# A hybrid decoder layer: inverse norms spread by transpositions, one partial sum of squares of x, and all steps in a new order

## The chip, the cores and the metric

The kernel runs on one core of a Trainium2 chip. The metric is the time of one execution on the device in microseconds (us). A core has a matrix engine (TensorE, in profile rows PE, with its weight loads as PEld), VectorE (DVE), ScalarE (ACT), GpSimd (POOL) and SyncE (SP), which here issues the DMA transfers. Each runs its own queue of instructions in order, and waits for the others by semaphores.

## The reference

One decoder layer over x (1 x 512 x 1024, float32): a normalised input goes through one combined projection, four heads of differential attention and eight heads of sparse attention in three branches run on it, their outputs are mixed by one projection and added to x, and a SwiGLU block with 2816 hidden columns follows.

```python
def rms_norm(x, g):
    y = xf * lax.rsqrt(jnp.mean(xf * xf, axis=-1, keepdims=True) + NORM_EPS)
    return (y * g.astype(jnp.float32)).astype(x.dtype)
...
    o_diff = diff_attention(dq, dk, dv, lam)
    o_diff = (rms_norm(o_diff, diff_subln) * (1.0 - lam_init)).reshape(B, S, DIFF_WIDTH)
...
        h = rms_norm(x, attn_pre_norm[l])
        mix = hybrid_mixer(h, ...)
        x = x + rms_norm(mix, attn_post_norm[l])
        h = rms_norm(x, ffn_pre_norm[l])
        f = (jax.nn.silu(h @ w_gate[l]) * (h @ w_up[l])) @ w_down[l]
        x = x + rms_norm(f, ffn_post_norm[l])
```

Two of these norms bear on the change: the first one, over the 1024 columns of x, and the one over the 128 columns of each differential head's output.

## The kernel before

*Number format.* Most products are float32 products made of three products of a reduced format (`fp32r`): each operand is split into a high part (ScalarE, `whi`, `xh`, `pth`) and a remainder (VectorE or GpSimd, `wlo`, `xl`, `ptl`), and high x high, high x low and low x high are summed in PSUM. A few small products are taken in float32 directly, `ssum`, `rb`, `rsb` and `ms` among them. `tr` (L867) transposes probabilities, `trc` (L1034) those of the compressed branch and `trh` (L1303) the normalised rows ahead of SwiGLU; these are `pe.transpose`.

*The stages, by the time of the profile.* Up to about 150 us: x comes in transposed (eight tiles of 128 columns by 512 tokens), is multiplied with the projection weights, and the results are rotated (rope) and written to DRAM for later. The pieces of the products of weight blocks 4 and 5 (`fm4`, `fm5`, L506) and the v products (`v`, L640) need no norm, since the norm's factor of a token is put in later: into the rope tables (`scale_rope`, L452) and into v (`dv`, L657/L660). From about 150 to 262 us the attention heads run, interleaved: D0 to D3 are differential, N0 to N7 sparse. Scores `sc` (L836 to L842), maxima `nm` (L846, DVE), exponentials `p` with their sums `l` (L850, ACT), inverses of `l` (L1007, DVE), gating of `l` and scaling of `p` (L1011, L1015, POOL), transposition, split into `pth` (L877, ACT) and `ptl` (L880, DVE), and the products with the values `avn` (L1046) or `av` (L925). Some output projections (`mixp`, L1113) are taken between, the last (`mix`, L1127) follow. From 262 to about 305 us come the norms around the residual, on VectorE above all (`pre`, L1273), while TensorE begins the SwiGLU products. From there to 622 us TensorE works through these (`yz` and `x`, L1380) and the down products (`acc`, L1454, L1602); weights stream in and are split. The last norm follows, to 635 us.

*The norm of x.* ScalarE squares x tile by tile in place (`square_x`, L392), and `add_x` (L395) sums the squares: the even tiles into the first and the odd tiles into the second, 6 additions of 128 x 512. `row_sums` (L440) lets TensorE sum each over the partitions, by products with a column of ones: for each of 4 blocks of 128 tokens two products, `ssum`. `row_norms` takes the inverse root (L294 to L303) to `rstd`, a column per token block. The factor must then stand along the rows of tiles in which tokens run along the free dimension: `row_spread` (L449) does it with 4 products of `rstd`, broadcast to 128 columns, and the identity, `rb`.

*The norm of a differential head.* Squares (`sq`), sums by `ms` (L939), `dr` (L943 on DVE, L971 on ACT, and `newton` on POOL, L947 to L950), and `spread` (L955), again 4 products with the identity, `rsb`. `ML` (L974) multiplies the output with it.

*The order.* Every step is a short function under a name, in `ops`. Three tables of such names (`PLAN`, `PLAN_NORM`, `PLAN_END`) give the order in which they are called, and that is the order of the instructions in each engine's queue:

```python
    plan = PLAN.split()
    assert sorted(plan) == sorted(ops), set(plan) ^ set(ops)
    ctx.enter_context(tc.manual_schedule())
    for tok in plan:
        ops[tok]()
```

In these names `xS3` is the square of x tile 3, `xA3` its addition, `rs` is `row_sums`, `rn` `row_norms`, `rb` `row_spread`, `F0.0` to `F0.2` the three products of weight block 0, `fh0` and `fl0` the split of its weights (L510, L515), and `D3RB` the spread of head D3. Buffers are given out from pools of fixed size (three weight tiles of each kind, for example), so the order also decides when a buffer becomes free.

Of the kernel before, what the change touches and what calls it, by code (L numbers as in the profile page):

```python
# [248 lines left out]
def hybrid_block_kernel(  # L249
# [144 lines left out]
    def add_x(k):  # L394
        dve.tensor_tensor(sqs[k % 2], sqs[k % 2], sqs[k], OP.add)  # L395
# [1526 lines left out]
```

## Time and profile before

| | us |
|---|---|
| median of 3 runs | 637.15 (636.68 to 637.2) |
| the profiled execution | 636.96 |
| its span | 635.1 |
| TensorE busy in it | 623.4 |
| VectorE busy | 549.7 |
| ScalarE busy | 373.6 |
| GpSimd busy | 97.6 |

The span is what the profiler shows of the instructions; 1.9 us of the execution lie around it. The mean granted clock of TensorE is 0.998 of full speed. In rows with "x8" that number counts records of instructions; a row's duration can overlap that of the next, since products are pipelined. The chain is followed back from the last instruction, at each step to what released it, and so its pieces add up to the span.

### The profile page before, as it was taken

How to read it: one execution, taken by the hardware profiler on the slowest of the kernel's cores; microseconds unless marked ns; L12 is line 12 of the kernel's file. 1: busy time of each engine (PE TensorE's matmuls, PEld its weight loads, DVE VectorE, ACT ScalarE, POOL GpSimd, SP SyncE). 2: the span in 40 equal slices, each digit the busy share in tenths (PEclk: the TensorE clock that was granted, in tenths of full speed). 3: DMA queues.
4: the chain of work that ended last, by engine and by line, in shares of the span. 5: the costliest groups of instructions: out<-in, count | busy, mean ns of one | idle time of the engine just before them, and what ended most of it. 6: DMA issues, size and time to landing. Idle time of an engine off the chain costs nothing.

```text
span 635.1 us, 11068 instructions
## 1 busy us (share of the span) xinstructions
PE 623.4 (98%) x4130; PEld 567.1 (89%) x4130; DVE 549.7 (87%) x965; ACT 373.6 (59%) x782; POOL 97.6 (15%) x151
## 2 busy tenths in 40 slices
PE   8999999999999999999999999999999999999995
PEld 5988888898899988888999999999999998888884
DVE  5599787989789875799999989899999999999877
ACT  6346357367788877567667555454554575566422
POOL 0200000006676868600000000000000000000000
PEclk9999999999999999999999999999999999999999
DMA  7567887453242314244133332445542554467603
GB/s 267 168 191 289 267 284 265 169 185 148 84 151 100 100 45 189 84 165 152 67 134 103 129 111 90 133 150 159 173 124 93 166 158 150 161 190 251 217 19 116
DMA packets 33045, 98.41 MB, mean 155 GB/s; under 512 B 4192, under 2 KB 5344, under 8 KB 32096
## 3 DMA queue, kind: packets, MB, share of 16 engines
q1 hardware_dynamic: 32992, 97.72, 45.9%
q8 instruction: 32, 0.52, 0.3%
q14 instruction: 21, 0.17, 0.1%
HBM read 82.10 MB, written 15.60 MB: 154 GB/s over the span
## 4 chain that ended last, share of the span: by engine, by line
PE 84%; DVE 9%; ACT 2%; issue 2%; POOL 1%; DMA 1%; SPq 0%; DVEq 0%; ACTq 0%; POOLq 0%
PE yz L1380 29%; PE acc L1454 14%; PE fm L523 12%; PE x L1380 4%; PE v L640 3%; PE acc L1602 3%; PE avn L1046 2%; PE tr L867 2%; PE g L640 2%; PE sc L836 2%; PE fm L506 2%; PE sc L837 2%; PE mixp L1113 1%; PE cmp L739 1%; DVE nm L846 1%
## 5 line engine op out<-in xcount | busy, mean ns | idle before, releaser
L850 ACT ACTIVATE p<-sc,nm 128x128 f32<-128x128 f32 (+3 forms) x96 | 50.4, 532 | 10.0 <-DVE nm L846 9.0
L846 DVE TENSOR_REDUCE nm<-sc 128x1 f32<-128x128 f32 (+3 forms) x96 | 43.8, 480 | 7.0 <-PE sc L842 5.3
L1380 PE MATMUL yz<-rope,wbh 128*128 128x256 f32 x352 | 49.0, 282 | 0.0
L1015 POOL TENSOR_TENSOR p<-p,l 128x256 f32<-128x256 f32 (+3 forms) x64 | 45.0, 726 | 0.9
L1380 PEld LDWEIGHTS yz<-rope,wbh 128*128 128x128 f32 x352 | 44.9, 189 | 0.0
L880 DVE TENSOR_TENSOR ptl<-tr,pth 128x384 fp32r<-128x384 f32 (+1 forms) x60 | 35.0, 596 | 9.4 <-ACT pth L877 9.0
L877 ACT ACTIVATE pth<-tr 128x384 fp32r<-128x384 f32 (+1 forms) x60 | 30.1, 529 | 10.1 <-PE tr L867 8.9
L836 PE MATMUL sc<-kst,qst 128*128 128x128 f32 (+3 forms) x96 | 32.6, 354 | 0.8 <-DVE ptl L880 0.4
L1357 ACT ACTIVATE weh<-e 128x1024 fp32r<-128x1024 f32 x22 | 23.3, 1058 | 15.7 <-DVE e L1339 15.2
L510 ACT ACTIVATE whi<-wraw 128x1024 fp32r<-128x1024 f32 x14 | 14.8, 1059 | 28.4 <-PE fm L523 15.7
L867 PE MATMUL tr<-ident,p 128*128 128x128 f32 x200 | 29.7, 274 | 0.8 <-POOL p L1015 0.8
L837 PE MATMUL sc<-kst,qst 128*128 128x128 f32 (+3 forms) x96 | 30.2, 322 | 0.0
L1365 DVE TENSOR_TENSOR wbl<-wraw,wbh 128x1024 fp32r<-128x1024 f32 x22 | 26.8, 1219 | 2.0 <-ACT wbh L1357 1.5
L1380 PE MATMUL yz<-rope,wbl 128*128 128x256 f32 x176 | 28.1, 282 | 0.0
L1365 DVE TENSOR_TENSOR wlo<-wraw,whi 128x1024 fp32r<-128x1024 f32 x22 | 26.7, 1219 | 1.6 <-ACT whi L1357 1.6
L523 PE MATMUL fm<-xh,whi 128*128 128x512 f32 x112 | 28.0, 393 | 0.0
L1390 ACT ACTIVATE snap<-yz 128x256 f32<-128x256 f32 x22 | 8.4, 384 | 33.0 <-PE yz L1380 32.9
L523 PE MATMUL fm<-xh,wlo 128*128 128x512 f32 x112 | 27.8, 390 | 0.0
L523 PE MATMUL fm<-xl,whi 128*128 128x512 f32 x112 | 27.8, 390 | 0.0
L1365 DVE TENSOR_TENSOR wel<-e,weh 128x1024 fp32r<-128x1024 f32 x22 | 26.8, 1217 | 0.9 <-ACT weh L1357 0.6
L1503 ACT ACTIVATE whi<-wraw 128x1024 fp32r<-128x1024 f32 x20 | 20.9, 1053 | 10.8 <-PE acc L1454 6.7
L1357 ACT ACTIVATE whi<-wraw 128x1024 fp32r<-128x1024 f32 x22 | 23.0, 1052 | 6.9 <-PE x L1380 4.8
(377 smaller groups left out, 1990.6 us busy)
## 6 DMA issues: line engine op xcount, KB each, us to landing
wraw<-in_wg SPq DMA_DIRECT2D x24, 512.0 KB, 3.4
wraw<-in_wu SPq DMA_DIRECT2D x22, 512.0 KB, 3.4
wraw<-in_wd SPq DMA_DIRECT2D x22, 512.0 KB, 3.6
wraw<-in_wf SPq DMA_DIRECT2D x14, 512.0 KB, 5.7
qk<-rope SPq DMA_DIRECT2D x7, 1024.0 KB, 5.3
kst<-qk SPq DMA_DIRECT2D x24, 256.0 KB, 4.2
wraw<-in_wo SPq DMA_DIRECT2D x8, 512.0 KB, 4.0
qst<-qk SPq DMA_DIRECT2D x16, 256.0 KB, 2.9
```

Source lines behind the costliest of these rows:

```text
L523: pe.matmul(st["fm", m], fms[m][w][:, k * P:(k + 1) * P], xx[k], start=(c == 0 and k == 0), stop=(c == 2 and k == NK - 1))
L836: pe.matmul(sv[i], lhs, kk[:, 0, :w], start=(n == 0), stop=False, skip_group_check=True)
L837: pe.matmul(sv[i], lhs, kk[:, 1, :w], start=False, stop=False, skip_group_check=True)
L846: dve.tensor_reduce(nm[i], sv[i], AX.X, OP.max, negate=True)
L850: act.activation(pp[i], sv[i], AF.Exp, bias=nm[i], accum_out=hs["l"][:, row, i:i + 1])
L867: pe.transpose(tr[:, n * P:(n + 1) * P], pp[i][:, j * P:(j + 1) * P], ident)
L880: dve.tensor_tensor(part(u, 1), tv[u], f32(part(u, 0)), OP.subtract)
L1015: pool.tensor_tensor(p, p, hs["l"][:, 1 + br, i:i + 1].to_broadcast(list(p.shape)), OP.mult)
L1357: act.activation(t[0], w[src], AF.Copy)
L1365: dve.tensor_tensor(t[1], W[f][PARTS[n][0]], f32(t[0]), OP.subtract)
L1380: pe.matmul(o, W[f][w][wi][:, k * P:(k + 1) * P], hop[h][hi][:, k * HS:(k + 1) * HS], start=(n < 3 and m == 0), stop=(m == 11), skip_group ...
L1454: pe.matmul(acc[t], a[x][:, t * P:(t + 1) * P], b[y], start=(first and n == 0), stop=(last and n == 2))
```

## The change

The two float32 products that spread a column by means of the identity become transpositions. The second partial sum of squares is added to the first on VectorE (a new step `xA1`), and `row_sums` needs one product for each token block. All three tables of the order are written anew.

```diff
     def add_x(k):
-        dve.tensor_tensor(sqs[k % 2], sqs[k % 2], sqs[k], OP.add)
+        j = k % 2 if k > 1 else 0
+        dve.tensor_tensor(sqs[j], sqs[j], sqs[k], OP.add)
...
-        if k > 1:
+        if k:
             op(f"xA{k}", add_x, k)
...
     def row_sums():
         st["ssum"] = ps("ssum")
         for i in range(NT):
-            for j in range(2):
-                pe.matmul(st["ssum"][:, i:i + 1], sqs[j][:, i * P:(i + 1) * P], ones, start=(j == 0), stop=(j == 1))
+            pe.matmul(st["ssum"][:, i:i + 1], sqs[0][:, i * P:(i + 1) * P], ones, start=True, stop=True)
...
     def row_spread():
-            pe.matmul(st["rb"][:, i * P:(i + 1) * P], rstd[:, i:i + 1].to_broadcast([P, P]), ident, start=True, stop=True)
+            pe.transpose(st["rb"][:, i * P:(i + 1) * P], rstd[:, i:i + 1].to_broadcast([P, P]), ident)
...
         def spread():
-                pe.matmul(hs["rb"][:, i * P:(i + 1) * P], hs["r"][3][:, i:i + 1].to_broadcast([P, P]), ident,
-                          start=True, stop=True)
+                pe.transpose(hs["rb"][:, i * P:(i + 1) * P], hs["r"][3][:, i:i + 1].to_broadcast([P, P]), ident)
...
 PLAN = """
-xS6 cc v0p2.1 v0p1.1 xS5 xA5 xS0 xA2 xS7 xA4 fL1 rL3 KP0 xA6 fL0 LW0 W0a xA7 rs F5.0.7 fh0 K21 F5.0.5 F4.1.5 rL2
+xA5 rL3 rL0 xA7 xA1 lL v0p3.1 v0p1.1 fh0 fl0 rs F0.0 F4.2.4
```

In the rows that follow, a name's number is that of a buffer's use, and "x4" four instructions alike; what is in a row's arrow is output and inputs.

TensorE's queue from the sums of squares to the first spread, before:

```order
L440 MATMUL ssum_413<-ones_90,xraw_160 128x1 x8
L506 MATMUL fm5_166<-xh7_312,whi_134 128x512
L506 MATMUL fm5_166<-xh5_296,whi_134 128x512
L506 MATMUL fm4_168<-xh5_296,wlo_175 128x512
L506 MATMUL fm5_166<-xl6_279,whi_134 128x512
L506 MATMUL fm5_166<-xh3_192,whi_134 128x512
L506 MATMUL fm4_168<-xh4_285,whi_158 128x512
L506 MATMUL fm4_168<-xh6_277,whi_158 128x512
L449 MATMUL rb_461<-ident_83,rstd_92 128x128 x4
L523 MATMUL fm0_466<-xh0_200,whi_423 128x512
L523 MATMUL fm0_466<-xh1_164,whi_423 128x512
```

and now (`fm0` is the first product of weight block 0, which stood behind the spread before):

```order
L440 MATMUL ssum_425<-ones_90,xraw_162 128x1 x4
L523 MATMUL fm0_430<-xh0_203,whi_421 128x512
L523 MATMUL fm0_430<-xh1_164,whi_421 128x512
L523 MATMUL fm0_430<-xh2_181,whi_421 128x512
L523 MATMUL fm0_430<-xh3_192,whi_421 128x512
L523 MATMUL fm0_430<-xh4_265,whi_421 128x512
L523 MATMUL fm0_430<-xh5_299,whi_421 128x512
L523 MATMUL fm0_430<-xh6_269,whi_421 128x512
L523 MATMUL fm0_430<-xh7_310,whi_421 128x512
L506 MATMUL fm4_172<-xl4_271,whi_160 128x512
L506 MATMUL fm4_172<-xh4_265,whi_160 128x512
L449 MATMUL rb_464<-ident_83,rstd_92 128x128 x4
```

Four products of sums instead of eight, and ten products instead of seven between these and the spread, eight of which need the high part of block 0's weights (`whi_421`); all of block 0's first product has moved ahead of the spread.

GpSimd's queue behind the last gate (`l`, L1011) of the last sparse head, up to the Newton steps of the last differential head, D3, before:

```order
L1015 TENSOR_TENSOR p_2971<-p_2971,l3_2850 128x128
L1015 TENSOR_TENSOR p_3303<-p_3303,l3_2850 128x256
L1015 TENSOR_TENSOR p_3110<-p_3110,l3_2850 128x384
L1015 TENSOR_TENSOR p_3301<-p_3301,l3_2850 128x384
L1015 TENSOR_TENSOR p_2957<-p_2957,l3_2850 128x256
L1069 TENSOR_TENSOR ol6_3277<-opair_3033,oh6_3276 128x512
L1015 TENSOR_TENSOR p_3296<-p_3296,l3_2850 128x512
L1015 TENSOR_TENSOR p_3294<-p_3294,l3_2850 128x128
L947 TENSOR_TENSOR dr_3362<-dr_3361 128x4
L948 TENSOR_TENSOR dr_3362<-dr_3362,dr_3360 128x4
L949 TENSOR_SCALAR dr_3362<-dr_3362 128x4
L950 TENSOR_TENSOR dr_3363<-dr_3361,dr_3362 128x4
```

and now (line numbers of this part are one less than before, since `spread` lost a line):

```order
L1014 TENSOR_TENSOR p_3318<-p_3318,l3_2865 128x256
L1014 TENSOR_TENSOR p_3321<-p_3321,l3_2865 128x384
L1014 TENSOR_TENSOR p_3323<-p_3323,l3_2865 128x128
L1014 TENSOR_TENSOR p_3314<-p_3314,l3_2865 128x512
L1100 TENSOR_TENSOR wl1_3423<-wraw_3134,wh1_3176 128x512
L1028 TENSOR_TENSOR pcs_3266<-pc_2952,pcs_3266 128x4x64
L947 TENSOR_TENSOR dr_3392<-dr_3391 128x4
L948 TENSOR_TENSOR dr_3392<-dr_3392,dr_3390 128x4
L949 TENSOR_SCALAR dr_3392<-dr_3392 128x4
L950 TENSOR_TENSOR dr_3393<-dr_3391,dr_3392 128x4
```

The gate is followed by four scalings instead of five and two, the remainder `wl` and the compressed branch's `pcs` (L1028, L1029 before) now stand ahead of the Newton steps, and an `ol` stands no longer there.

TensorE's queue around the spread of D3, before:

```order
L1046 MATMUL avn_3428<-pth_3395,vn0_1571 128x512
L1046 MATMUL avn_3428<-ptl_3396,vn0_1571 128x512
L955 MATMUL rsb_3437<-ident_83,dr_3363 128x128 x4
L867 MATMUL tr_3443<-ident_83,p_3303 128x128
L867 MATMUL tr_3443<-ident_83,p_3301 128x128
L867 MATMUL tr_3443<-ident_83,p_3296 128x128
L1034 MATMUL trc_3449<-ident_r_84,pcs_3338 128x128 x4
L1046 MATMUL avn_3428<-pth_3395,vn1_1613 128x384
L1046 MATMUL avn_3428<-ptl_3396,vn1_1613 128x384
L1046 MATMUL avn_3428<-pth_3395,vn2_1568 128x256
L1046 MATMUL avn_3428<-ptl_3396,vn2_1568 128x256
L1046 MATMUL avn_3428<-pth_3395,vn3_1562 128x128
```

and now:

```order
L1045 MATMUL avn_3355<-ptl_3343,vn2_1548 128x256
L1045 MATMUL avn_3355<-pth_3342,vn3_1523 128x128
L1045 MATMUL avn_3355<-ptl_3343,vn3_1523 128x128
L867 MATMUL tr_3425<-ident_83,p_3323 128x128
L867 MATMUL tr_3425<-ident_83,p_3318 128x128
L867 MATMUL tr_3425<-ident_83,p_3321 128x128
L867 MATMUL tr_3425<-ident_83,p_3314 128x128
L1033 MATMUL trc_3433<-ident_r_84,pcs_3266 128x128 x4
L955 MATMUL rsb_3442<-ident_83,dr_3393 128x128 x4
L1045 MATMUL avn_3447<-pth_3403,vn0_1464 128x512
L1045 MATMUL avn_3447<-ptl_3404,vn0_1464 128x512
```

The spread stood ahead of the last three transpositions and those of `pcs` (`trc`), behind the first two products of the last `avn`; now it stands behind all transpositions and ahead of all products of the last `avn`.

More of the change, by code (lines that the diff above doesn't have):

```diff
@@ new lines @@
+sum_ff.6.2 sum_ff.6.4 sums.3 high_ff.5.e low_ff.1.d block.1.4 high_ff.5.d high_ff.6.e low_ff.6.e low_ff.5.e
+high_ff.7.a block.5.6 high_ff.4.d gate_c.1 mult.1 snap_1.6 sum_x.6 sum_ff.6.3 low_ff.7.a high_ff.6.b block.5.5
+block.7.1 snap_1.7 sums.2 block.6.5 low_ff.5.d block.7.2 block.6.6 load_ff.7.u sum_ff.7.1 sum_ff.7.3 low_ff.6.b
+load_ff.8.g high_ff.7.b low_ff.7.b block.3.4 snap_2.5 block.5.3 sum_ff.7.2 low_ff.2.d sum_ff.7.4 snap_2.6
+high_ff.7.e block.6.3 high_ff.7.d sums.4 high_ff.6.d block.2.4 low_ff.7.e block.7.6 high_ff.8.a load_ff.8.u
@@ new lines @@
+low_ff.7.d low_ff.8.a sum_ff.8.1 sum_ff.8.2 sum_ff.8.4 sum_x.7 block.5.7 sum_ff.8.3 block.8.1 high_ff.8.e low_ff.8.e
+load_ff.9.g load_ff.9.u high_ff.9.a low_ff.9.a high_ff.8.b low_ff.8.b gate_c.2 snap_1.8 gate_c.0 block.6.7 gate_c.3
+mult.2 block.8.6 block.8.5 snap_2.8 sums.5 block.5.4 sum_ff.9.1 sum_ff.9.3 sum_ff.9.2 sum_ff.9.4 low_ff.6.d
+high_ff.9.b low_ff.4.d block.7.5 load_ff.10.g low_ff.9.b snap_2.7 gate_c.5 sums.6 load_ff.10.u load_ff.11.u
+sum_ff.10.1 gate_x.3 sum_ff.10.2 gx.0 mult.0 block.4.4 sum_ff.10.4 block.8.2 block.9.1 high_ff.10.a low_ff.10.a
@@ new lines @@
+block.5.2 block.7.3 pair_sums.0.1 block.6.4 pair_sums.0.3 high_ff.9.e high_ff.8.d snap_1.9 low_ff.9.e block.9.5
+block.9.6 block.9.2 gate_c.6 load_ff.11.g block.10.1 sum_ff.10.3 block.7.7 block.8.3 sum_ff.11.1 sum_ff.11.2
+high_ff.11.a high_ff.10.e block.8.7 sum_ff.11.3 snap_2.9 block.9.7 sum_ff.11.4 high_ff.11.b high_ff.11.d gate_c.4
+block.9.3 gate_x.6 low_ff.11.a low_ff.10.e sum_x.9 block.10.2 low_ff.11.b mult.3 pair_sums.0.2 snap_1.10 block.10.5
+gate_x.4 load_ff.12.g high_ff.12.a sums.7 block.10.6 low_ff.12.a block.12.1 high_ff.10.b low_ff.10.b mult.4
@@ new lines @@
+high_ff.12.d sum_ff.14.2 high_ff.10.d high_ff.13.e sum_ff.14.3 sum_ff.14.4 block.12.7 pair_sums.1.4 sum_x.11
+snap_2.11 block.11.3 low_ff.13.e sum_x.12 high_ff.14.b low_ff.14.b gate_x.8 block.13.1 block.13.5 high_ff.14.a
+block.12.3 low_ff.14.a mult.6 gate_c.8 mult.8 high_ff.13.b gate_x.5 mult.5 pair_sums.2.1 sums.9 pair_sums.2.2
+snap_1.13 load_ff.15.g block.11.7 high_ff.14.e high_ff.15.a block.13.6 snap_2.13 block.9.4 load_ff.15.u low_ff.13.b
+block.14.1 load_ff.16.u sum_x.10 sum_ff.15.1 sum_ff.15.2 sum_ff.15.3 gate_x.7 sum_ff.15.4 low_ff.15.a block.13.7
@@ new lines @@
+high_ff.18.b low_ff.17.e block.15.3 block.17.1 snap_1.17 low_ff.17.b low_ff.18.b low_ff.16.d sums.16 sum_x.14
+gate_x.14 mult.13 high_ff.18.e low_ff.18.e block.12.4 pair_sums.4.3 gate_c.12 block.17.5 block.17.6 load_ff.19.g
+load_ff.19.u sum_ff.19.1 sum_ff.19.2 gate_x.12 sum_ff.19.3 high_ff.19.a low_ff.19.a mult.12 sum_ff.19.4 block.18.1
+sums.15 high_ff.19.b low_ff.19.b block.16.4 block.18.2 snap_1.18 block.18.6 block.18.5 snap_2.17 block.17.3
+block.17.7 high_ff.17.d low_ff.17.d gate_c.16 sum_x.18 load_ff.20.g low_ff.14.d high_ff.20.a pair_sums.2.3
@@ new lines @@
+left_a.2.1.0 snap_2.18 block.18.3 block.18.7 load_ff.20.u sum_ff.20.1 sum_ff.20.2 sum_ff.20.3 high_ff.20.b
+sum_ff.20.4 pair_sums.6.1 low_ff.20.a block.20.1 high_ff.19.e low_ff.19.e pair_sums.3.3 low_ff.15.d block.19.1
+block.19.5 high_ff.20.e load_ff.21.g high_ff.21.a sums.14 low_ff.20.e block.15.4 load_ff.21.u sum_ff.21.1
+sum_ff.21.2 low_ff.21.a snap_1.19 sum_ff.21.4 pair_sums.6.2 block.19.6 mult.16 block.14.4 low_ff.20.b snap_2.19
+block.19.3 high_ff.21.e low_ff.21.e gate_c.14 sum_x.15 gate_x.15 mult.14 sum_x.17 block.21.1 high_ff.21.d
```

321 lines of the change are left out of this document (146 added, 175 removed).

## The prediction

> **What bounds the kernel now.** I read the busy shares and the chain first, then TensorE's waits, then the windows. From the page:
>
> ```profile
> PE 623.4 (98%) x4130; PEld 567.1 (89%) x4130; DVE 549.7 (87%) x965; ACT 373.6 (59%) x782; POOL 97.6 (15%) x151
> PEclk9999999999999999999999999999999999999999
> PE 84%; DVE 9%; ACT 2%; issue 2%; POOL 1%; DMA 1%; SPq 0%; DVEq 0%; ACTq 0%; POOLq 0%
> ```
>
> TensorE is busy for 98% of the span and is 84% of the chain, at full clock in every slice. Whether a removed product shortens the run therefore hangs on whether TensorE was waiting near it. TensorE's waits (total us, times, longest):
>
> ```profile
> PE fm L506 <- ACT xh L381: 1.1, 1, 1.1
> PE tr L867 <- POOL p L1015: 0.8, 1, 0.8
> PE sc L836 <- DVE ptl L880: 0.4, 1, 0.4
> PE avn L1046 <- ACT p L850: 0.2, 1, 0.2
> PE avn L1046 <- DVE ptl L880: 0.2, 1, 0.2
> PE trh L1303 <- DVE pre L1273: 0.2, 1, 0.2
> ```
>
> The first is the start, the others sum to 1.8 us. The windows say where (stretch, its length, busy us of each engine, clock, DMA):
>
> ```profile
> 0.00:30.00 30.00, 27.73 (x164) 22.56 (x165) 16.45 (x33) 16.09 (x24) 4.63 (x8) 1.00 0.69 230
> 150.00:200.00 50.00, 48.95 (x371) 45.02 (x369) 42.00 (x100) 39.66 (x122) 33.66 (x54) 1.00 0.34 117
> 200.00:250.00 50.00, 49.85 (x351) 45.80 (x351) 38.91 (x96) 40.80 (x122) 39.47 (x59) 1.00 0.32 111
> 250.00:300.00 50.00, 49.19 (x276) 42.46 (x275) 42.65 (x84) 33.03 (x71) 13.63 (x19) 1.00 0.39 137
> 300.00:622.00 322.00, 321.79 (x2281) 302.20 (x2281) 296.85 (x445) 177.41 (x296) 0.00 (x0) 1.00 0.42 138
> ```
>
> The first pair is length and TensorE's busy time: between 30 us and 622 us it is idle for about 2.2 us (1.05, 0.15, 0.81 and 0.21). So TensorE work taken out before 300 us comes off the end almost one for one, and a new order can win at most those 2.2 us, but has no such limit on what it can lose.
>
> **The change part by part.** A row of a spread product and of the transposition that takes its place (by form: count | busy, mean ns), and then the stretches of all of them on the chain (start, us, records):
>
> ```profile
> L867 PE MATMUL tr<-ident,p 128*128 128x128 f32 x200 | 29.7, 274 | 0.8 <-POOL p L1015 0.8
> L955 PE MATMUL rsb<-ident,dr 128*128 128x128 f32 x32 | 4.2, 275 | 0.0
> ...
> 29.47 1.68 PE ssum L440 x16
> 31.14 1.70 PE fm L506 x7
> 32.84 0.90 PE rb L449 x8
> 165.77 0.76 PE tr L867 x7
> 170.59 0.89 PE rsb L955 x8
> 243.20 1.22 PE tr L867 x11
> 257.77 0.89 PE rsb L955 x8
> ```
>
> The means include pipeline overlap (275 ns for one that is followed 110 ns later), so I price by the chain. The code issues 4 products for `rb` and the trace has 8 records: a full float32 product is two records. A transposition of a float32 tile is one record (0.76/7 = 0.109 us), whereas a spread of four products takes 0.89 or 0.90.
>
> *Sums of squares.* 8 products become 4, 16 records become 8. 1.68/16 = 0.105 us each, so 8 x 0.105 = 0.84 us less. *First spread:* 0.90 becomes 4 x 0.109 = 0.44, so 0.46 less. *Four head spreads:* each 0.89 - 0.44 = 0.45, together 1.8 less. All lie in TensorE's own row with no wait of its own: 0.84 + 0.46 + 1.8 = 3.1 us.
>
> *The extra addition.* VectorE gets a seventh 128x512 addition and then does the first weight remainder (`wlo`, L515) and the small steps to `rstd`:
>
> ```profile
> 17.45 0.68 DVE L395 TENSOR_TENSOR xraw<-xraw 128x512 f32<-128x512 f32 x1
> 30.11 1.23 DVE L515 TENSOR_TENSOR wlo<-wraw,whi 128x1024 fp32r<-128x1024 f32 x1 [3.54 <-ACT whi L510]
> 31.48 0.16 DVE L295 TENSOR_SCALAR rr<-ssum 128x4 f32<-128x4 f32 x1
> 32.31 0.16 DVE L303 TENSOR_TENSOR rstd<-rr 128x4 f32<-128x4 f32 x1
> 29.02 1.06 ACT L510 ACTIVATE whi<-wraw 128x1024 fp32r<-128x1024 f32 x1 [6.72 <-PE v L640]
> ```
>
> It costs 0.68 us in 3.54 us of idle time: nothing, and 0.68 if that cover were gone (ScalarE's squares would have to end 2.9 us later).
>
> *What stands between the sums and the first spread.* Before: 7 products, 1.70 us, while the path from the sums to `rstd` takes 31.14 to 32.47 plus the release. Now: 10 products, 10 x 1.70/7 = 2.4 us. But the sums end 0.84 us earlier, whereas `wlo` still ends at 31.34, and `rr` (L295) is queued behind it: `rstd` can be ready no earlier than about 32.4. One more `fm` product than before stands ahead of the sums, so they end near 31.14 - 0.84 + 0.23 = 30.5, and the spread is reached at 32.9. It is ready by 0.4 us or so. The other tie: the first of those ten needs `whi` of L510, which ends at 30.08, and TensorE reaches it at 30.5. Both hold; if either fails it eats at most the 0.84 (all of the sums' gain). I take 0.
>
> *The heads' spreads at the end of attention.* This is where TensorE waited for GpSimd before (start, us, engine, and in brackets the idle time before it):
>
> ```profile
> 250.10 0.20 POOL L1011 TENSOR_TENSOR l<-l,gates 128x4 f32<-128x4 f32 x1 [0.96 <-DVE l L1007]
> 250.25 3.11 POOL L1015 TENSOR_TENSOR p<-p,l 128x128 f32<-128x128 f32 x5
> 245.14 2.76 POOL L1015 TENSOR_TENSOR p<-p,l 128x512 f32<-128x512 f32 x4
> 256.76 0.20 POOL L950 TENSOR_TENSOR dr<-dr 128x4 f32<-128x4 f32 x1
> 256.92 0.74 POOL L1029 TENSOR_TENSOR pcs<-pc,pcs 128x256 fp32r<-128x256 f32 x1
> 257.60 1.28 POOL L1101 TENSOR_TENSOR wl<-wraw,wh 128x512 fp32r<-128x512 f32 x1
> 253.42 0.55 PE L867 MATMUL tr<-ident,p 128*128 128x128 f32 x3 [0.81 <-POOL p L1015]
> 257.61 1.05 PE L955 MATMUL rsb<-ident,dr 128*128 128x128 f32 x8
> ```
>
> Before, after the gate (`l`, L1011) GpSimd did five scalings, an `ol`, two scalings and the four Newton steps: 250.25 to 256.96, 6.7 us until `dr` of D3. Now it does four scalings of the same four widths as the row of x4 (2.76), a `wl` (1.28), a `pcs` (0.74) and the Newton steps (255.92 to 256.96 in the trace, 1.04): 5.8 us. The gate still waits for VectorE, GpSimd having been idle for 0.96 us. TensorE behind the last scaling now has 8 transpositions (0.87), eight products of probabilities (1.23 on the chain), 4 transpositions (0.44) and 4 of `pcs` (about 0.4): it arrives at `rsb` 2.9 us after the scalings, 5.7 after the gate. That is level with 5.8, so 0.1 to 0.3 us can appear there; the 0.8 us wait at the scalings can go, since the last scaling needs 2.76 and not 3.11. Ends: 0.8 less, 0.8 more. I take 0.3 less.
>
> *All other steps.* Their instructions are the same in number, in another order on every queue, SP's loads included. At the start one of the three dummy products (`warm`) now stands ahead of the first real one, behind the wait of 1.1 us that both orders have; all three remain, and I take 0, with 0.23 (1.70/7) either way. In the attention stage, the small waits of 0.2 to 0.4 us in the list above are ties between VectorE, ScalarE and TensorE, and their neighbours are now others. I take 0.1 less, with ends at 1.4 less (all other idle time gone) and, upwards, three more waits like the largest, 2.4. Behind attention, two rows say what the gain must pass:
>
> ```profile
> 303.61 0.67 DVE pre L1273
> 309.97 30.06 PE yz L1380 x252
> ...
> DVE e L1337 <- DMA wraw<-in_wu: 2.4, 5, 0.7
> ```
>
> The norms end on VectorE (`pre`), whose work starts from attention's end and shifts with it. From there on VectorE is busy for 297 of 322 us and waited 2.4 us for loads without TensorE feeling it (0.21 us idle): 25 us are free to take up a moved load. I take 0 for that stage, with the 2.4 of that row as the end upwards.
>
> *Sum.* 3.1 + 0.3 + 0.1 = 3.5 us off the profiled execution's 636.96 is 633.5; the median of the runs is 0.2 above that execution, so 633.6.
>
> A rule of the Trainium skill speaks against the change: "TensorE: Matmul & The Clock Gate", Part 4: PE-mode transpose, says that the clock gate's full state does not engage for transpositions, as they do not count as TensorE being busy in the same way. By that rule a longer run of transpositions would be followed by matmuls at half the clock. The trace does not agree for runs of this length: it holds 200 transpositions of probabilities among its products, up to eleven in a row, at a granted clock of 1.00 in every window above.
>
> **The rivals.**
>
> *A wait takes the place of the work (slower).* The one place where it could is the last gate of attention. Everything that TensorE still has to do there stands behind the last head's scalings, so each us that the gate comes later relative to TensorE is a us of the run. For it: GpSimd is 39 of 50 us busy in the window before, its order is new, and TensorE arrives 3 us sooner. Against it: GpSimd was idle for 0.96 us before that gate, its order there is shorter, and VectorE and ScalarE, on which the gate waits, have about a fifth of the window free. Eating the gain takes 3.1 us of new wait: 637; it is slower beyond the 0.2% (1.3 us) that a measurement can tell from 4.4 us on: 638.5 and more. A backlog of 2 to 4 us, four to five scalings, gives 635.9 to 638.
>
> *The head of the program hides its part.* If `rstd` is bound by `wlo` and `whi` instead of by the sums, the 0.84 and 0.46 go into a wait ahead of the first spread, and 1.8 to 2.2 remain: 635.0 to 635.4. For it: `rr` stands right behind `wlo`. Against: ten products cover it.
>
> *The order wins as well.* All waits between 150 us and 300 us go: 3.1 + 1.9 gives 632.1. For it speak only the windows.
>
> *Transpositions are cheaper still.* A spread of a column could take a quarter of 0.89, 0.22, instead of 0.44: 5 x 0.22 = 1.1 us more, 632.5. The row of `tr` speaks against it: 0.109 us for one, against 0.89/4 = 0.223 for a full product, is a factor of two. The Trainium skill, "TensorE: Matmul & The Clock Gate", section Terms, gives the transpose mode as four times faster for float32.
>
> *The change doesn't do it.* The transposed column is broadcast to 128 columns by a stride of zero; if such a tile were still taken in two records, only the sums' 0.84 and the order remain: 636. No row shows a transposition of a broadcast column.
>
> **How the numbers follow.** Forecast, between 632.9 and 634.6: 0.52. Head hidden or small new waits, 634.6 to 635.9: 0.19. Order wins or cheaper transpositions, below 632.9: 0.12. New waits eat most of it, or the transpositions stay double, 635.9 to 638.4: 0.12. Slower, above 638.4: 0.05. So faster by over 0.2% (below 635.9) is 0.83, within 0.2% 0.12, slower 0.05. The range reaches from 631.8 (nearly all idle time gone) to 636.4 (2.8 us of new waits, or double transpositions).
>
> **What would show it.** `ssum` with 8 records and about 0.84 us; `rb` with 4 records and `rsb` with 16, a spread near 0.44; VectorE's idle time ahead of L515 near 2.9; no wait of TensorE before `rb`, and at most 0.3 before the last `rsb`; TensorE's idle time between 100 us and 300 us at 2 us or less; the part after 310 us as long as before. I am wrong if TensorE's waits in the attention stage sum to over 3 us, or a spread takes over 0.6.

## The result and the profile after

| | before | after |
|---|---|---|
| median, us | 636.91 (636.65 to 637.2, 4 runs) | 630.62 (630.22 to 632.29, 4 runs) |
| ratio | | 0.9906, 95% interval 0.9894 to 0.9917 |
| profiled execution, us | 636.96 | 630.22 |
| its span, us | 635.1 | 628.1 |

The change makes the kernel faster by 6.3 us, 0.94%. The forecast was 3.5 us off and 633.6, with a range of 631.8 to 636.4; the time lies 1.2 us below that range. The sign was right, the size was not.

The page after, in the lines that the prediction showed of before:

```profile
PE 618.7 (99%) x4102; PEld 561.1 (89%) x4102; DVE 549.3 (87%) x966; ACT 374.5 (60%) x782; POOL 99.3 (16%) x151
PEclk9999999999999999999999999999999999999998
PE 90%; DVE 6%; ACT 1%; DMA 1%; issue 1%; DVEq 0%; ACTq 0%
```

TensorE's records are fewer by 28: 8 of `ssum`, 4 of `rb`, 16 of `rsb`. Its busy time fell by 4.7 us, its share of the chain rose from 84% to 90%, VectorE's fell from 9% to 6%. TensorE's waits after, all of them, and the products of the change (by form):

```profile
PE warm L364 <- DVE warm L361: 1.2, 1, 1.2
PE yz L1379 <- DVE rope L1295: 0.5, 1, 0.5
PE tr L867 <- ACT p L850: 0.2, 1, 0.2
PE sc L836 <- DVE opair L1059: 0.2, 1, 0.2
...
L955 PE MATMUL rsb<-ident,dr 128*128 128x128 f32 x16 | 2.4, 275 | 0.0
L440 PE MATMUL ssum<-ones,xraw 128*128 128x1 f32 x8 | 0.9, 239 | 0.0
L449 PE MATMUL rb<-ident,rstd 128*128 128x128 f32 x4 | 0.6, 272 | 0.0
```

Neither `rb` nor `rsb` waits, and of the waits in attention two of 0.2 us are left. The windows after (length, TensorE's busy time, then the other engines, clock, DMA):

```profile
140.00:170.00 30.00, 29.90 (x235) 27.80 (x235) 27.66 (x68) 23.96 (x75) 21.27 (x38) 1.00 0.37 123
150.00:200.00 50.00, 49.90 (x390) 46.11 (x388) 43.76 (x109) 43.20 (x131) 34.48 (x56) 1.00 0.33 106
200.00:250.00 50.00, 49.56 (x344) 43.86 (x343) 37.15 (x88) 40.74 (x118) 43.49 (x65) 1.00 0.20 65
250.00:300.00 50.00, 50.00 (x288) 43.85 (x287) 46.81 (x90) 33.30 (x70) 6.73 (x7) 1.00 0.51 179
```

and of before one more window:

```profile
140.00:170.00 30.00, 29.05 (x219) 26.20 (x218) 25.77 (x64) 22.57 (x72) 16.95 (x33) 1.00 0.44 156
```

Between 140 and 170 us TensorE is busy for only 0.85 us more than before, and does 16 records more. At 0.11 to 0.23 us each (the spacings below) that is 1.8 to 3.7 us of work: before, much waiting lay inside what is counted as busy. The timeline of before shows how:

```profile
150.80 0.23 PE L994 MATMUL scc<-cmask_b,ident_b 128*128 128x128 bf16 x1
151.45 0.30 PE L836 MATMUL sc<-kst,qst 128*128 128x128 f32 x1 [0.42 <-DVE ptl L880]
...
158.66 0.39 PE L1046 MATMUL avn<-ptl,vn 128*128 128x512 f32 x1
158.90 0.34 PE L1046 MATMUL avn<-pth,vn 128*128 128x384 f32 x1
...
161.05 0.34 PE L842 MATMUL sc<-mask_b,ident_b 128*128 128x128 bf16 x2
161.21 0.50 PE L1046 MATMUL avn<-pth,vn 128*128 128x512 f32 x1
161.93 0.50 PE L1046 MATMUL avn<-ptl,vn 128*128 128x512 f32 x1 [0.22 <-DVE ptl L880]
```

Unhindered, a product of 512 columns is followed by the next after 0.24 us (158.66 to 158.90), although its own record lasts 0.39. At 161.21 the next one starts after 0.72. The delay is about 0.48 us, the idle time shown only 0.22; and at 151.45 the next starts 0.65 after a mask product, with 0.42 shown as idle (two mask products at 161.05 let the next one start after 0.16).

So I measured TensorE's delay instead of its idle time: for each record, the start of the next minus its own, less the usual spacing of its shape (512 columns 0.227 us, 384 0.176, 256 0.119, 128 0.109; the 40th percentile over the traces of before and after). Work, the sum of these spacings, and delay add up to the time from the first product to the last. The table gives the delay in us by windows of each kernel's own time, and the work.

```
kernel                      0-10 10-30 30-50 50-140 140-170 170-250 250-260 260-310 310-end  delay   work
before                       1.1   0.0   0.2   1.5    3.3     2.5     1.0     0.7     1.9     12.2  614.4
after                        0.8   0.0   0.2   1.3    0.9     2.8    -0.1     0.2     2.2      8.3  611.3
edits, old order             0.7   0.1   1.1   1.5    3.3     2.7     1.1     0.7     1.9     13.1  611.3
new order, old products      0.9   0.0   0.1   1.2    0.6     2.3     0.0     0.2     2.1      7.5  614.4
head spreads only            1.1   0.0   0.2   2.7    3.3     2.8     1.0     0.8     1.9     13.7  612.6
row edits only               1.0   0.0   1.1   1.6    3.3     2.5     1.1     0.7     2.4     13.6  613.1
new head, then old           1.1   0.0   0.2   1.2    4.5     4.1     1.0     0.7     1.9     14.7  611.3
old head, then new           1.0   0.0   1.1   1.6    5.1     5.0    -0.1     0.6     1.9     16.1  611.3
old, v products spread       1.1   0.0   0.2   1.6    4.8     4.5     0.9     0.7     1.9     15.7  614.4
new, v products in a lump    1.1   0.0   0.2   1.2    4.2     3.2    -0.1     0.2     2.7     12.6  611.3
```

The work fell by 3.1 us, the delay by 3.9: by 2.4 between 140 and 170 us, by 1.1 where TensorE waited for GpSimd at 253 us, by 0.5 in the norms. Together that is the 7.0 us between the profiled spans; the medians differ by 6.3, as the profiled execution after had the shortest time of its four.

The differences in this table are firm, the level of the delay is not. With the 25th, 50th or 60th percentile as the usual spacing the delay of before would be 18.1, 7.1 or 4.5 us, since each of 4,100 records then has a few ns more or less; the fall from before to after stays at 3.9, and 2.3 to 2.5 of it lie between 140 and 170 us. A count that hangs less on it takes single delays of more than 0.1 us alone, from 30 us on: before has 19 of them, 5.1 us in all, with 2.2 us shown as idle; after has 11, 2.5 us, with 1.0 shown; the new order with the old products has 6, 1.4 us, with 0.6 shown. Two rows (new head then old, new with v products in a lump) hold 1.3 and 1.5 us in a stretch of half the granted clock, which is no waiting (last section).

### The profile page after: what moved, and what is told of

Same layout as the page of the kernel before. It is cut to its first block, busy times and chain, and to the rows that moved or that the text cites. A ratio compares the mean times of both kernels' runs of the same rounds, so it can differ in the third digit from the quotient of the medians.

```text
span 628.1 us, 11018 instructions
## 1 busy us (share of the span) xinstructions
PE 618.7 (99%) x4102; PEld 561.1 (89%) x4102; DVE 549.3 (87%) x966; ACT 374.5 (60%) x782; POOL 99.3 (16%) x151
## 4 chain that ended last, share of the span: by engine, by line
PE 90%; DVE 6%; ACT 1%; DMA 1%; issue 1%; DVEq 0%; ACTq 0%
PE yz L1379 26%; PE acc L1453 14%; PE fm L523 12%; PE mix L1126 4%; PE x L1379 4%; PE v L640 4%; PE tr L867 3%; PE avn L1045 3%; PE acc L1601 3%; PE sc L836 2%; PE sc L837 2%; PE g L640 2%; PE mixp L1112 2%; PE fm L506 2%; PE cmp L739 1%; PE warm L364 1%
## 5 line engine op out<-in xcount | busy, mean ns | idle before, releaser
L850 ACT ACTIVATE p<-sc,nm 128x384 f32<-128x384 f32 (+3 forms) x96 | 50.0, 527 | 11.9 <-DVE nm L846 10.4
L846 DVE TENSOR_REDUCE nm<-sc 128x1 f32<-128x512 f32 (+3 forms) x96 | 43.5, 481 | 8.0 <-PE sc L842 6.2
L1356 ACT ACTIVATE wbh<-wraw 128x1024 fp32r<-128x1024 f32 x22 | 23.2, 1056 | 14.1 <-DVE wraw L1343 9.8
L836 PE MATMUL sc<-kst,qst 128*128 128x128 f32 (+3 forms) x96 | 30.8, 338 | 0.4 <-DVE opair L1059 0.2
L837 PE MATMUL sc<-kst,qst 128*128 128x128 f32 (+3 forms) x96 | 30.7, 322 | 0.0
L1356 ACT ACTIVATE whi<-wraw 128x1024 fp32r<-128x1024 f32 x22 | 23.1, 1056 | 11.7 <-DMA wraw<-in_wg 10.8
L1502 ACT ACTIVATE whi<-wraw 128x1024 fp32r<-128x1024 f32 x20 | 21.1, 1059 | 13.4 <-PE acc L1453 6.2
L1364 DVE TENSOR_TENSOR wlo<-wraw,whi 128x1024 fp32r<-128x1024 f32 x22 | 26.8, 1217 | 0.2 <-ACT whi L1356 0.2
L1508 DVE TENSOR_TENSOR wlo<-wraw,whi 128x1024 fp32r<-128x1024 f32 x20 | 24.1, 1219 | 1.7 <-ACT whi L1502 1.6
```

What stands on the lines that cost most here:

```text
L836: pe.matmul(sv[i], lhs, kk[:, 0, :w], start=(n == 0), stop=False, skip_group_check=True)
L837: pe.matmul(sv[i], lhs, kk[:, 1, :w], start=False, stop=False, skip_group_check=True)
L846: dve.tensor_reduce(nm[i], sv[i], AX.X, OP.max, negate=True)
L850: act.activation(pp[i], sv[i], AF.Exp, bias=nm[i], accum_out=hs["l"][:, row, i:i + 1])
L1356: act.activation(t[0], w[src], AF.Copy)
L1364: dve.tensor_tensor(t[1], W[f][PARTS[n][0]], f32(t[0]), OP.subtract)
```

## The experiments

All run on the chip with the kernel before beside them; its median was 637.0 to 637.2 in each group, and the ratios are to that.

**The edits without the order, and the order without the edits.** The first has the code after, with the tables of before and `xA1` put in (a piece of `PLAN`):

```diff
-xS7 xA4 fL1 rL3 KP0 xA6 fL0 LW0 W0a xA7 rs F5.0.7 fh0
+xS7 xA4 fL1 rL3 KP0 xA6 fL0 LW0 W0a xA7 xA1 rs F5.0.7 fh0
```

> All edits (transpositions for rb and rsb, one sum of squares with its seventh addition right behind the sixth), but the three tables of the order as before. Theory A (edits and order add up): 3.1 us off, about 633.8, the records of ssum 8, rb 4 and rsb 16, and TensorE's hidden and open waits as before. Theory B (in the old order part of the freed time turns into new waits, and only the new order frees it): 1 to 2.5 us off, 634.4 to 635.9. Theory C (the edits bring more than their own TensorE time, since they end waits of others): 4 us off or more.

Measured: 635.41 us, ratio 0.9978 (0.9967 to 0.9988), 1.6 us off by the medians and 2.2 in the profile (span 632.9). The work fell by 3.1 us, but between 30 and 50 us there is 0.9 us of new delay, with these waits of TensorE:

```profile
PE rb L449 <- DVE rstd L303: 0.3, 1, 0.3
PE fm L523 <- DVE wlo L515: 0.2, 1, 0.2
```

Theory B holds. The second has the code before, and the new tables without `xA1`:

> The three new tables, but the full float32 products for rb and rsb and two partial sums of squares as before (without the seventh addition). Theory A: the order alone brings what is left of the 6.3 us, 3.2 off, about 633.7. Theory B: it brings more than that, 3.8 to 5. Theory C: it brings 2.3 or less.

Measured: 633.51 us, ratio 0.9942 (0.9927 to 0.9956), 3.5 off. (The profiled execution took the shortest time of the four, 632.49, and its span of 630.4 is 4.7 off.) The number is nearest to theory A's 3.2; the interval reaches from 2.8 to 4.7 off and so into theory B. The edits are worth 1.6 us in the old order and 633.51 - 630.62 = 2.9 in the new one (2.3 by the profiled spans).

**Which edit loses in the old order.** The head spreads alone (`spread` changed, nothing else), and everything but them:

> The kernel before with the transposition in the four head spreads (rsb) alone; old order, two sums of squares, full products for rb. Theory: their TensorE time, 1.8 us, comes off, about 635.2 (ratio 0.9972), and TensorE loses nothing new around 30 to 40 us. Rival (the old order turns part of it into waits in attention): 0.5 to 1 us off, 636.0 to 636.5.

> The kernel before with the transposition in the first spread (rb) and one sum of squares (with the seventh addition behind the sixth); old order, full products for the head spreads. Theory: of their 1.3 us of TensorE time 0.7 to 0.9 turn into waits for rstd and wlo between 30 and 50 us, 0.4 to 0.6 off, 636.4 to 636.6, not to be told from no change. Rival (all of it arrives): 1.3 off, 635.7.

Measured: 636.23 us, ratio 0.9987 (0.9978 to 0.9996), 0.8 off; and 637.09, 1.0002 (0.9993 to 1.0011), nothing. The second fits the theory's mechanism: of 1.3 us of work 0.9 comes back as delay between 30 and 50 us (the table), and the interval excludes the rival's 1.3; of the 0.4 to 0.6 that were to be left it reaches only the lower part. The first has the rival's number (0.5 to 1 off), but not its reason. In its profile the 1.75 us of work are gone and attention's delay is about as before (3.3, 2.8, 1.0 against 3.3, 2.5, 1.0), but between 100 and 110 us, ahead of all head spreads, TensorE waited once for a load:

```profile
PE sc L836 <- DMA kst<-qk: 0.9, 1, 0.9
```

The row was not in the traces of before or of the edits in the old order. Its eleven runs lie between 635.4 and 637.2, so this wait may come and go; that was not tried.

**The spread moved in the old order.**

```diff
-F4.0.6 rL0 v0d3 rb F0.0
+F4.0.6 rL0 v0d3 F0.0 rb
```

> All edits in the old order, but the first spread stands behind the first product of weight block 0, so that 15 products instead of 7 lie between the sums of squares and the spread. Theory: the 0.74 us that TensorE lost in 30 to 40 us with all edits in the old order (a wait for rstd of 0.3 and one for wlo of 0.2 among them) go, 0.6 to 0.8 below that kernel (635.4), about 634.7. Rival (the products behind the spread wait for the rope tables instead): the same as it, 635.2 to 635.6.

Measured: 636.65 us, ratio 0.9992 (0.9983 to 1.0001), 1.2 us more than without the move. The wait for `rstd` went (delay in 30 to 40 us 0.19 instead of 0.89), and a larger one took its place:

```profile
41.66 2.12 PE L523 MATMUL fm<-xh,wlo 128*128 128x512 f32 x8 [1.36 <-DVE wlo L515]
...
34.87 0.69 DVE L452 TENSOR_TENSOR ckv<-rb,ckv 128x512 f32<-128x512 f32 x1 [0.74 <-PE rb L449]
40.39 1.22 DVE L515 TENSOR_TENSOR wlo<-wraw,whi 128x1024 fp32r<-128x1024 f32 x1
```

On VectorE's queue the rope tables, which need `rb`, stand ahead of the next weight remainder. The later spread holds them up, and with them `wlo`. Both theories fall. The new order has a `wlo` ahead of the tables (the changed kernel's VectorE queue):

```profile
32.05 0.17 DVE L444 TENSOR_SCALAR nrstd<-rstd 128x4 f32<-128x4 f32 x1
32.13 1.22 DVE L515 TENSOR_TENSOR wlo<-wraw,whi 128x1024 fp32r<-128x1024 f32 x1
33.26 0.68 DVE L452 TENSOR_TENSOR skv<-rb,skv 128x512 f32<-128x512 f32 x1
```

So the ten products between the sums and the spread go with a change on another queue; a later spread alone makes it worse. That the two belong together is read off the queues; the pair was not tried in the old order.

**Which table.** `PLAN_END` is empty in both kernels, so two tables are new: `PLAN` up to the end of attention, and `PLAN_NORM` for the norms and SwiGLU. The new `PLAN` with the old `PLAN_NORM`, and the reverse:

> The changed kernel with its new PLAN (everything to the end of attention), but the old tables PLAN_NORM and PLAN_END. If the order's gain lies in the attention stage, where the end of attention came 6.9 us earlier in the profile and the end of the program 7.0: within 0.5 us of the changed kernel, 630.6 to 631.1. If the norms' and the SwiGLU stage's order matter: 1 us or more behind it, 631.6 or above.

> All edits with the old PLAN (and the seventh addition), but the new PLAN_NORM and PLAN_END. By the theory that the order's gain is the attention stage's: as with all tables old, about 633.8 under theory A, within 0.5 us of it. If the tail's order brings something: 1 us less than with all tables old.

Measured: 630.64 us, ratio 0.9903 (0.9889 to 0.9918), the changed kernel's time; and 635.33, 0.9977 (0.9966 to 0.9988), that of the old order with all edits. By the medians the order's whole gain is in `PLAN`. The new `PLAN_NORM` is not without effect: it takes 0.4 to 0.5 us of delay out of the norms, but with it 0.6 to 0.7 us of delay stand between 310 and 350 us, where there is hardly any with the old one.

**Is VectorE the bound at 145 to 162 us?** The chain of before is on VectorE for three quarters of that stretch, by its summary:

```profile
by line: DVE nm L846 23.8%; DVE ptl L880 20.5%; DVE p L913 8.0%; ACT pth L877 5.9%; DVE pc L1019 4.7%; DVE pc L999 4.0%; DVE pc L1004 3.9%; issue 3.9%; DVE nmc L1001 3.5%; DVE vcs L801 3.4%; PE avn L1046 2.9%; DVE dv L660 2.8%; ACT dv L657 
```

Steps were left out, in the old order, as a control elsewhere, and in the new order:

```diff
+    for n in ("D1MX0", "D1MX1", "D1MX2", "D1MX3", "N1CM"):
+        del ops[n]
     plan = PLAN.split()
```

> The kernel before, old order and old products, without five VectorE steps that ran between 154 and 163 us: the four mixes of head D1 (its two probability maps are not combined) and one scaling of the compressed branch of N1. In the profile they took 2.1 to 2.6 us, and the chain there ran on VectorE from 145 to 162 us, while TensorE fell 3.4 us behind its own rate (start to start). Theory V (VectorE is the bound in this stretch, and the order matters because of it): 1.7 to 2.6 us off, 634.4 to 635.3. Rival (TensorE is the bound, the chain's VectorE pieces are only ties): 0 to 0.6 us off.

> Control: the kernel before without the same five VectorE steps of D3 and N6, 2.1 to 2.6 us around 236 us, where the chain is TensorE's and TensorE fell behind by 0.4 us in ten. Theory V: 0 to 0.5 us off. Rival (VectorE's work matters everywhere in attention): 1.7 us off or more, like D1.

> The changed kernel without the same five VectorE steps as in the run on the old order (the four mixes of D1, one scaling of N1), 2.1 to 2.6 us. Theory: TensorE hardly waits for VectorE there any more in the new order (0.9 us of delay from 140 to 170 us against 3.3): 0 to 0.4 off, 630.2 to 630.6. Rival (VectorE is the bound of the stretch in the new order as well): 1 us off or more.

Measured: 636.56 us, ratio 0.9991 (0.9982 to 1.0001); 637.26, 1.0005 (0.9995 to 1.0014); and 630.79, 0.9908 (0.9895 to 0.9922). In the old order only the delay right behind the steps shrank (160 to 170 us: from 1.28 to 0.54), 0.5 us by the medians where theory V wanted 1.7 or more. Theory V falls. In the new order VectorE is even busier between 140 and 170 us (27.66 us against 25.77), and less work for it changes nothing. So it isn't how much VectorE has to do; that its results are there earlier for what TensorE does next is the reading that is left, and no run tests it by itself.

**Halves of the order.** Up to the v products at 178 us in one order, behind them in the other (all edits in both):

> All edits; the steps that the old PLAN has up to 178 us stand in the order in which the new PLAN has them, the rest of attention and the tail as in the old tables. Theory: most of the order's gain is that the VectorE stretch at 145 to 162 us is gone: 2.5 to 3.5 us below the old order with all edits (635.4), 632 to 632.9. Rival (the gain is at the end of attention or spread over it): less than 1.5 us below, 633.9 or above.

> All edits; up to 178 us the old order, and behind it the remaining steps of attention in the new PLAN's order. Theory: only the end of attention's 0.8 to 1.0 us (TensorE's wait for GpSimd at 253 us) is won: 634.4 to 634.7 against 635.4. Rival (the later part of attention has the gain): 2.5 us below or more, under 632.9.

Measured: 636.69 us, ratio 0.9991 (0.9982 to 1.0001); and 639.75, 1.0042 (1.0029 to 1.0056). Each half shows its own part: with the new head the delay from 140 to 160 us is 0.41 instead of 2.05, with the new end that from 250 to 260 us is -0.1 instead of 1.0. But at the seam from 160 to 180 us 5.6 and 5.2 us of delay appear, where the old order has 1.5. About half of it is one wait for GpSimd in each:

```profile
PE rsb L954 <- POOL dr L949: 2.7, 1, 2.7
PE trc L1032 <- POOL pcs L1027: 2.5, 1, 2.5
```

With the new head, GpSimd ended `dr` at 169.97 us, as in the kernel before (169.98); TensorE came earlier and waited for it. Behind this wait its clock was halved for a stretch, which holds another 1.3 us of the 5.6 (last section); the one of the ten executions that had a mean clock of 0.997, and not 0.994 or 0.995, took 634.96 us. So cut at this place neither half brings its part; other places were not tried, and a part of both times is the clock.

**Single moves in the old order.** GpSimd's scalings at the end of attention, with TensorE's queue unchanged:

```diff
 L1015 TENSOR_TENSOR p<-p,l_2850 128x128
-L1015 TENSOR_TENSOR p<-p,l_2850 128x256
-L1015 TENSOR_TENSOR p<-p,l_2850 128x384 x2
-L1015 TENSOR_TENSOR p<-p,l_2850 128x256
+L1015 TENSOR_TENSOR p<-p,l_2850 128x384
+L1015 TENSOR_TENSOR p<-p,l_2850 128x256 x2
+L1015 TENSOR_TENSOR p<-p,l_2850 128x384
```

> The kernel before, old products and old order but for one place: behind the last gate of attention two scalings on GpSimd (N7's, 256 and 384 wide, 0.61 and 0.83 us) stand behind the scaling for which TensorE waited at 253 us, instead of ahead of it. TensorE's queue is the same. Theory O (such single ties are what the new order removed, and what they take off comes off the end): the wait at 253 us and TensorE's 1.0 us of delay in 250 to 260 us go, 0.8 to 1.0 us off. Rival (the wait moves on to the next transpositions or into the norms behind attention): 0 to 0.3 us off.

Measured: 636.98 us, ratio 0.9993 (0.9984 to 1.0002). TensorE's wait for GpSimd is gone from its list, the delay from 250 to 260 us fell from 0.96 to 0.49: half of what theory O wanted. The time is the rival's, not to be told from no change. Then with it the later spread, and `KF1` (L801) behind `N0L00` (the split of probabilities at 151 us), all edits in the old order:

> All edits in the old order with three steps moved: the spread as in the run beside, the two scalings as in the run beside, and the remainder of the compressed values (L801, 0.59 us on VectorE) behind the split of the probabilities for which TensorE waited at 151 us (0.61 us of delay). Theory O: the three add up, 0.7 + 1.0 + 0.5 below all edits in the old order (635.4): 633.0 to 633.4. Rival (each wait that is removed makes room for the next): 634 to 635.

Measured: 635.9 us, ratio 0.998 (0.9972 to 0.9989), no better than without the moves, and above what theory and rival wanted. The later spread cost 1.2 us in the run before, so the two other moves bring about 0.75 beside it by the medians (636.65 - 635.9). Where `KF1` was moved nothing was won on balance: the delay of 0.61 at 151 us shrank to about 0.39 (in three pieces) and that of 0.41 at 158 us to 0.30, while those at 157 and 160 us grew from 0.17 and 0.25 to 0.42 and 0.36.

**The v products as cover.** The chains show a plain difference: products of v (L640), which read weights and x alone, stand in lumps of 24 in the old order and in groups of 12 in the new one (before, then after):

```profile
142.41 2.88 PE v L640 x24
162.89 2.88 PE v L640 x24
175.73 2.95 PE v L640 x24
```

```profile
139.94 1.49 PE v L640 x12
142.36 1.49 PE v L640 x12
152.18 1.48 PE v L640 x12
155.88 1.48 PE v L640 x12
```

The lump at 163 us was split in the old order, the two groups at 152 and 156 us were put together in the new one:

```diff
 old: D1E01 N1SC +v1p1.0 N2S00 ... N1X13 +v1p1.1 N0V00 ... N1PH -v1p1.0 ... -v1p1.1 v1a1
 new: -v1p1.0 ... -v1p1.1 ... +v1p1.0 +v1p1.1 v1a1
```

> The kernel before, old products and old order, but the lump of 24 v products at 163 us is split: 12 stand ahead of the scores for which TensorE waited at 151 us, 12 ahead of the avn product for which it waited at 158 us. The other queues keep their order. Theory F (cover: products that need no other engine, spread between the attention steps, take up the time in which TensorE waits for VectorE and ScalarE): the delay of 0.6 and 0.4 us there and most of 0.25 and 0.5 behind go, 1.0 to 1.7 off, 635.3 to 636.0. Rival (the stretch is bound by VectorE's chain, the waits only come later): 0 to 0.4 off.

> All edits in the old order with two changes of place: the v products as in the run beside, and GpSimd's two scalings of N7 later, as in the earlier run. Theory F: 635.4 less 1.0 to 1.7 less about 0.5, 633.2 to 633.9. Rival: 634.6 or above.

> The changed kernel with the opposite move: the two groups of 12 v products at 152 and 156 us put together into one lump of 24 behind, where the second half's consumer follows. Theory F: TensorE's delay between 150 and 165 us rises from 0.5 by 0.8 to 1.6 us, 631.4 to 632.2. Rival (the new order's other changes carry it): within 0.4 of the changed kernel, 630.3 to 631.0.

Measured: 641.42 us, ratio 1.006 (1.0048 to 1.0073), 4.2 slower; 638.37, 1.0021 (1.0012 to 1.003); and 633.31, 0.9936 (0.9922 to 0.9949), 2.7 slower than the changed kernel.

In the new order the groups do cover: without them the delay from 140 to 170 us rises from 0.9 to 4.2, more than theory F wanted, and 1.5 of it lies in a stretch of half the clock in the profiled execution (634.6 us, mean clock 0.994). The three executions with a mean clock of 0.996 or 0.997 took 632.82 to 633.31, still 2.2 to 2.7 more than the changed kernel. In the old order theory F falls. TensorE there stops at the v product itself:

```profile
150.91 0.23 PE L994 MATMUL scc<-cmask_b,ident_b 128*128 128x128 bf16 x1
151.56 0.71 PE L640 MATMUL v<-whi,xh 128*128 128x256 f32 x4 [0.41 <-DVE ptl L880]
```

It reads nothing of `ptl`; by the code it can wait for that step only to get its PSUM tile, since all of TensorE's outputs take turns in one pool (`ps`). The scores that stood there before read nothing of `ptl` either and waited as long (0.42), so by this reading whatever product stands at this place meets the wait. The v product then holds its tile until `v1a1`, longer than in the lump, and the delay from 170 to 180 us rises from 0.18 to 2.0. That the held tile is the reason for this rise is argued from the code and not shown.

**One step swapped in the new order.** The wait of 0.5 us for L1295 (at 320 us):

```diff
-L1336 TENSOR_TENSOR e<-wraw 128x512
 L1295 TENSOR_TENSOR rope<-s_4167,rope 128x4x128
+L1336 TENSOR_TENSOR e<-wraw 128x512
```

> The changed kernel with one pair of VectorE steps swapped: at 320 us the remainder of a left operand (L1295), for which TensorE waited 0.5 us (0.63 us of delay), stands ahead of the sum (L1336) that waits for a weight load. Theory O: 0.5 to 0.7 us below the changed kernel (630.6), about 630.0, and the wait of TensorE for L1295 gone. Rival: TensorE waits for the next remainder instead, same as the changed kernel.

Measured: 629.81 us (629.48 to 630.08, 4 runs), ratio 0.9883 (0.987 to 0.9897). The wait is gone from the list and the delay from 310 to 350 us fell from 0.72 to 0.06, as theory O wanted. This is the fastest kernel tried; its interval still meets that of the changed kernel at the edge, so that it is faster than that one rests on the trace and not on the time alone.

## Why the prediction was wrong

**Right:** the price of the edits. 3.1 us of TensorE work were forecast and 3.1 are gone: `ssum` takes 0.79 us on the chain instead of 1.68, a spread four times 0.11. In the new order 2.9 of it arrives by the medians, in the old one only 1.6; that "TensorE work taken out before 300 us comes off the end almost one for one" holds in the new order alone.

```profile
29.40 0.79 PE ssum L440 x8
...
248.31 1.33 PE tr L867 x12
...
251.46 0.62 PE L955 MATMUL rsb<-ident,dr 128*128 128x128 f32 x4
251.84 0.47 PE L1045 MATMUL avn<-pth,vn 128*128 128x512 f32 x1
```

From the first record of the last spread to the next product it is 0.38 us. No row had shown a broadcast column transposed; it is one record, as forecast. Float32 records of 1, 64 and 128 columns follow each other after 0.111, 0.111 and 0.109 us in these traces, so what the transposition saves is the second record. The Trainium skill, "Perfetto Trace Analysis", section Transposes, wants logical transposes issued as transposes since they skip arithmetic; the rows agree. They show a factor of two, and not the four that the Trainium skill gives in "TensorE: Matmul & The Clock Gate", section Terms. The clock was not affected by the transpositions: 1.00 in the windows of the changed kernel, with twelve of them on the chain in a row at 248 us (1.33/12 = 0.111 us each).

**Right:** the head's ties and the last spread. `rb` and `rsb` wait for nothing. The rival "the head hides its part" is real, but in the old order (0.9 us of 1.3 lost), where seven products cover, and not in the new one.

**Wrong:** "a new order can win at most those 2.2 us", and with it the terms of 0.3 and 0.1. The step that failed was to take TensorE's idle time for its lost time. The order alone brought 3.5 us by the medians and 4.7 by the profiled spans, past the limit. The single delays of more than 0.1 us were 5.1 us where 2.2 were shown as idle, and between 140 and 170 us, where 0.95 was shown as idle, 2.4 us of delay went. The chain had given a sign of it: in this stretch most of its pieces are VectorE's and ScalarE's, and I priced only the waits that the list names. The Trainium skill, "Perfetto Trace Analysis", section Identifying the Most-Contended Engine, warns that matmul busy time is no good measure of how near TensorE is to its limit; here TensorE of the kernel before was busy for 48.95 of the 50 us from 150 to 200 us, and its single delays of more than 0.1 us there were 2.7 us.

**Right in place, wrong in size:** the last gate of attention. The prediction took 0.3 less for it, since TensorE would reach the last spread level with GpSimd; the delay from 250 to 260 us fell by 1.1. GpSimd was as forecast, 6.0 us from the gate to the end of `dr` where 5.8 were worked out:

```profile
244.51 0.21 POOL L1010 TENSOR_TENSOR l<-l,gates 128x4 f32<-128x4 f32 x1
250.28 0.20 POOL L950 TENSOR_TENSOR dr<-dr 128x4 f32<-128x4 f32 x1
```

TensorE was put too early: it reached the spread at 251.46, 7.0 us after the gate and not 5.7, so that no wait was left to pay. The 0.1 for all other steps was a choice without a row behind it, and most of the missed gain lay there: in the old order the single moves did not add up (what one wait lost, others took on in part or whole), while the new order changes the queues of VectorE, GpSimd and TensorE together.

**Open:** how much of the 2.4 us is due to the groups of v products. In the new order their place is worth 2.7 us by the medians, a part of it by the clock, and spread in the old order they cost 4.2, so the shares of the moves don't add up to a sum. The rest of what makes the new order better between 140 and 170 us was not found by a single move.

## What to carry to other kernels

Measure an in-order engine's loss from start to start against the usual spacing of the same shape; idle time between overlapping records shows only the tail of each wait. Compare kernels by it, and do not read its level. A saving on the bound engine arrives only where the neighbours' queues keep their lead: look at what each of them has queued between the freed step and its next user. Products that need no other engine's data can cover waits, as in the new order here; where the product itself waits, as in the old one, look at whose PSUM tile it gets before moving it.

## What the runs showed of the hardware

A wait can cost TensorE its clock, in one execution and not in another. With the v products in a lump, it was busy for 1.67 of 2.4 us, and then the granted clock was 0.54 for 3.6 us:

```profile
155.00:157.40 2.40, 1.67 (x8) 0.90 (x7) 2.40 (x6) 2.23 (x9) 1.74 (x3) 0.98 0.97 271
157.40:161.00 3.60, 3.60 (x19) 3.51 (x18) 1.07 (x5) 0.59 (x4) 1.60 (x3) 0.54 0.82 311
161.00:165.00 4.00, 3.75 (x31) 3.30 (x30) 1.83 (x4) 2.34 (x9) 1.32 (x4) 1.00 0.00 1
```

That is 3.6 x 0.46 = 1.7 us of the clock beside the waits. From start to start TensorE was 1.5 us late in this stretch: a product of 256 columns was followed by the next after 0.213 us instead of 0.119. The new head with the old end shows the same behind its wait of 2.7 us for GpSimd:

```profile
165.00:170.00 5.00, 2.20 (x13) 1.39 (x12) 3.55 (x7) 3.14 (x11) 4.75 (x12) 0.95 0.00 0
170.00:175.00 5.00, 4.98 (x28) 4.81 (x29) 1.64 (x4) 1.63 (x4) 5.00 (x5) 0.71 0.01 3
```

Again that is 5 x 0.05 + 5 x 0.29 = 1.7 us of the clock, and TensorE was 1.3 us late in it. The old head with the new end waited 2.5 us for GpSimd, and its profiled execution kept the clock (mean 0.999, 637.97 us); its six other executions had means of 0.992 to 0.995 and took 639.15 to 641.79. Of the old order with its v products spread, three executions had 0.998, the profiled one with its larger waits among them, and two 0.994. So the length of the wait alone does not decide it, and the medians of these kernels hold the clock as well as the waits. The Trainium skill, "TensorE: Matmul & The Clock Gate", section What's actually happening, describes such a gate: half clock after an idle window of about 3.4 us that runs free of the kernel. The length agrees: the granted clock was 0.50 from 157.28 to 160.69 us, 3.41 us. That a window runs free would fit the difference between executions, but no run shows it. The wait ahead was much shorter than such a window, as TensorE was busy for 2.68 of the 3.41 us before.

The first 10 us vary: TensorE's delay there was between 0.5 and 1.7 us over the profiles of the old order, whose first steps are the same. Whether that makes the scatter between runs of one kernel was not tried.
